# First-layer attention weights: a third exponential, and the remainder taken from the PSUM bank

## The chip, the cores and the metric

The kernel runs on one core of a Trainium2 chip. The metric is device time in microseconds (us) of one execution. The engines that matter are TensorE (PE in the profile, its weight loads PEld), VectorE (DVE), ScalarE (ACT), GpSimd (POOL) and SyncE (SP, which issues the transfers). Each runs its own instructions in the order in which they stand, and waits for others by semaphores. SBUF is the large working memory; PSUM has eight banks, into which TensorE writes its products, here each 128 partitions by 512 fp32 columns.

## The reference, cut to what matters

A two-layer encoder trunk for 2048 new frames and 32 sample frames, 1024 wide, all in fp32. The change lies in layer 0, 16 heads of 64, where a frame sees its own chunk of 64 and the eight chunks before it:

```python
s = jnp.einsum('bqhd,bkhd->bhqk', q, k).astype(jnp.float32) * scale
s = s + bias[None]                                  # clipped relative-position bias
s = jnp.where(mask[None, None], s, NEG_INF)
p = jax.nn.softmax(s, axis=-1).astype(v.dtype)
return jnp.einsum('bhqk,bkhd->bqhd', p, v)
```

Queries and keys are RMS-normalised per head before; the output is gated by silu(z) and projected. Layer 1 (latent attention) follows and is untouched.

## The kernel before

TensorE multiplies operands of a rounded fp32 kind. To keep fp32 accuracy the kernel splits every operand into a high part (rounded) and a low part (the remainder), and issues three products, or two where one side needs no split (`mm3`, lines 187 to 191).

Layer 0 is a run of 32 steps: two halves of the sequence, in each eight groups of two heads, in each two blocks of 512 queries. One step works on scores and values of a (group, block) while the projections, transposes and row maxima of the next are laid between them. `place` gives each piece a position in the step, and a scheduler that builds the program settles the order of the instructions on every engine from its own account of when things are ready; so an edit of one line can move neighbours on all engines.

Scores come in tiles of 128 keys by w queries (w = 128, 256, 384 or 512, each equally often). In block 0 a head has four tiles, in the blocks 1 to 3 eight: 8 groups x 2 heads x (4 + 3 x 8) = 448 tiles, 112 of each width. One tile goes through these steps (`scores`, `values`):

- two matmuls (lines 629 and 630) write the scores into a PSUM bank with the tag `st`. There are two such banks, used in turn (bank_74 and bank_78 in the built program), so tile i+2 needs the bank of tile i;
- VectorE adds the bias in the bank (633 or 636), or writes the mask (637);
- ScalarE takes exp twice from the bank: `P`, fp32 in SBUF (643), and `Ph`, the rounded high part (644);
- VectorE forms the low part `Pl` = `P` - `Ph` (645), all three in SBUF;
- GpSimd adds `P` to the running sum of the row, `acc` (647). For a head's first tile `P` is `acc` itself;
- two matmuls by the values, `Ph` first (656), then `Pl` (657), into a bank with the tag `av`, of which there is one (bank_94). In the program's text they stand two tiles behind the scores (`LAGA`), and the scheduler moves them on.

Beside this, VectorE also takes row maxima (595, 613), reciprocals for the softmax gate (687), splits of weights (429, 441) and of keys and queries (566, 567), and the sums that take the finished values out of the `av` bank (667, after ScalarE's copy 666). ScalarE copies the projections out of their banks (481, 513). In layer 1 a similar tile (`scores` of that layer) adds `P` to a sum that lies in a PSUM bank (1563), or, for a unit's second tile, adds two tiles that lie in SBUF.

Of the kernel before, what the change touches and what calls it, by code (L numbers as in the profile page):

```python
# [10 lines left out]
AF = mybir.ActivationFunctionType  # L11
ALU = mybir.AluOpType
# [19 lines left out]
def f32(ap):  # L32
    return ap if ap.dtype == F32 else ap.bitcast(F32)
# [6 lines left out]
def flip(t, c0, c1):  # L40

    n = t.shape[1]
    a = t[:, n - c1:n - c0]
    return bass.AP(a.tensor, a.offset + c1 - c0 - 1, [list(a.ap[0]), [-1, c1 - c0]])
# [55 lines left out]
def trunk(ctx: ExitStack, tc: tile.TileContext, I, O, stop=99):  # L100
    nc = tc.nc
    V, S, G, T = nc.vector, nc.scalar, nc.gpsimd, nc.tensor
# [90 lines left out]
    def bank(tag):  # L193
        order = psum[tag if tag in psum else "mx"]
        order.append(order.pop(0))
        return banks[order[-1]]
# [144 lines left out]
    def at1(shape, name, dt=F32, bufs=1):  # L341
        return at.tile(shape, dt, tag=name, name=name, bufs=bufs)
# [279 lines left out]
    def scores(s, h, n, c, t):  # L622
        blk, u = s["blk"], s[h]
        src = blk % 2 if c else 1 - blk % 2
        q0, w = (128 * t, 512 - 128 * t) if c else (0, 128 * t + 128)
        ks, qs = slice(128 * t, 128 * t + 128), slice(q0, q0 + w)
        bt = bias[s["g"], h][1]
        st = bank("st")
        T.matmul(st[:, 0:w], KA[h][src][:, ks], u["qa"][:, qs], start=True, stop=False)  # L629
        T.matmul(st[:, 0:w], KG[h][src][:, ks], u["qg"][:, qs], start=False, stop=True)  # L630
        if c:
            b1 = min(256, w)
            V.tensor_tensor(st[:, 0:b1], st[:, 0:b1], flip(bt, 0, b1), ALU.add)  # L633
        else:
            if t == 3:
                V.tensor_tensor(st[:, 0:128], st[:, 0:128], flip(bt, 128, 256), ALU.add)
            V.memset(st[0:64, w - 64:w], NEG)  # L637
        Ph = at1([128, 512], "Ph", F32R, PBUFS)
        Pl = at1([128, 512], "Pl", F32R, PBUFS)
        if n == 0:  # L640
            u["acc"] = at1([128, 512], "acc", bufs=2)
        P = at1([128, 512], "P", bufs=PBUFS) if n else u["acc"]
        S.activation(P[:, 0:w], st[:, 0:w], AF.Exp)  # L643
        S.activation(Ph[:, 0:w], st[:, 0:w], AF.Exp)
        V.tensor_tensor(Pl[:, 0:w], P[:, 0:w], f32(Ph[:, 0:w]), ALU.subtract)
        if n:
            G.tensor_tensor(u["acc"][:, qs], u["acc"][:, qs], P[:, 0:w], ALU.add)  # L647
        return Ph, Pl, w, qs, src
# [289 lines left out]
    for si, s in enumerate(steps):  # L938
# [55 lines left out]
        for i, (h, n, c, t) in enumerate(items):  # L994
            fifo.append((s, h, n, n == len(tiles) - 1, t, scores(s, h, n, c, t)))
            while plan and plan[0][0] <= (i + 1) / len(items):
                next(plan.pop(0)[1], None)
            if len(fifo) > LAGA:
                x = fifo.pop(0)
                values(*x)  # L1000
                if x[3]:
                    evac(x[0], x[1])
# [723 lines left out]
    for i in range(len(items) + LAG + 20):  # L1726
        if i < len(items):
            u, t = items[i]
            fifo.append((u, t, scores(u, t)))
# [233 lines left out]
```

## Time and profile before

| | us |
|---|---|
| median of 3 runs | 3889.08 (3886.15 to 3892.15) |
| profiled execution, device time | 3874.33 |
| its span, first to last instruction | 3872.2 |
| PE busy in the span | 3598.0 (93%) |
| DVE busy | 3023.3 (78%) |
| ACT busy | 2016.7 (52%) |
| POOL busy | 1622.4 (42%) |

The first tile of layer 0 reaches ScalarE at 127 us, and the last tile's work ends at about 1655 us; the stretch 125 to 1655 us is called the stage below. Times in rows are of the one profiled execution. A matmul's duration includes its way through the array: the next one begins before it ends, so busy time of PE is not PE at its peak.

### The profile page before, as it was taken

To read this page: it belongs to the slowest core of one execution; us is meant where nothing else is said; L and a number is where in the kernel's file an instruction comes from. 1 tells how busy PE (TensorE), PEld (TensorE's weight loads), DVE (VectorE), ACT (ScalarE), POOL (GpSimd) and SP (SyncE) were. 2 spreads that over 40 slices of the span, in tenths; PEclk is the share of its full clock that TensorE was granted. 3 is DMA by queue.
4 is the path that set the end of the run, shared out by engine and by line. 5 is a ranking of instruction groups with operands and counts; after the bars stand their busy time and mean duration, and the time that the engine had idled before them with its cause. 6 is when DMAs were issued, how large, how long until landed. Compare 5 with 4: busy or idle time off the path is not lost.

```text
span 3872.2 us, 56118 instructions
## 1 busy us (share of the span) xinstructions
PE 3598.0 (93%) x17410; PEld 2831.9 (73%) x17410; DVE 3023.3 (78%) x6646; ACT 2016.7 (52%) x4854; POOL 1622.4 (42%) x1680
## 2 busy tenths in 40 slices
PE   7899999889999999899999999889999999998999
PEld 4788888767766777677878888666767667766887
DVE  4788988889988888876777766788888888784663
ACT  4444544655544444542234555566766667664542
POOL 0222223333333323441013444377777777774032
PEclk9899999989999999799999999889999999998999
DMA  5222222222233332354453666652323323223253
GB/s 175 64 58 60 72 77 59 78 80 67 63 104 96 94 92 78 117 182 130 131 173 126 194 192 193 177 153 69 84 70 83 87 73 84 61 76 102 88 175 126
DMA packets 445036, 412.96 MB, mean 107 GB/s; under 512 B 72392, under 2 KB 367356, under 8 KB 437696
## 3 DMA queue, kind: packets, MB, share of 16 engines
q1 hardware_dynamic: 444736, 409.37, 36.2%
q8 instruction: 138, 2.26, 0.3%
q14 instruction: 162, 1.33, 0.1%
HBM read 251.72 MB, written 140.10 MB: 101 GB/s over the span
## 4 chain that ended last, share of the span: by engine, by line
PE 61%; DVE 20%; ACT 6%; issue 5%; DMA 4%; POOL 3%; SPq 0%; ACTq 0%; DVEq 0%; POOLq 0%
PE bank L189 10%; PE bank L190 10%; PE bank L191 10%; PE bank L1512 3%; PE bank L1537 3%; PE bank L1539 3%; PE bank L1538 3%; PE bank L1573 2%; PE bank L1572 2%; DVE ez@69_1247 L687 2%; PE bank L1592 1%; PE bank L656 1%; PE bank L657 1%; PE bank L629 1%; PE bank L591 1%
## 5 line engine op out<-in xcount | busy, mean ns | idle before, releaser
L1513 DVE TENSOR_REDUCE mp@319_16907<-bank 128x1 f32<-128x512 f32 (+3 forms) x384 | 235.1, 616 | 63.7 <-PE bank L1512 61.4
L647 POOL TENSOR_TENSOR acc@61_858<-acc@61_858,P@63_885 128x256 f32<-128x256 f32 (+3 forms) x64 | 57.2, 894 | 212.7 <-ACT P@63_885 L643 110.8
L1513 DVE TENSOR_REDUCE mp@320_16908<-bank 128x1 f32<-128x512 f32 (+1 forms) x192 | 115.7, 619 | 20.2 <-PE bank L1512 16.2
L643 ACT ACTIVATE P@63_885<-bank 128x384 f32<-128x384 f32 (+3 forms) x128 | 52.7, 412 | 126.0 <-DVE bank L633 62.1
L647 POOL TENSOR_TENSOR acc@61_858<-acc@61_858,P@64_886 128x256 f32<-128x256 f32 (+3 forms) x64 | 57.4, 898 | 143.4 <-ACT P@64_886 L643 99.7
L687 DVE RECIPROCAL ez@69_1247<-ez@69_1247 128x128 f32<-128x128 f32 x128 | 116.0, 922 | 0.0
L647 POOL TENSOR_TENSOR acc@61_858<-acc@61_858,P@65_887 128x128 f32<-128x128 f32 (+3 forms) x64 | 57.2, 894 | 139.5 <-ACT P@65_887 L643 94.8
L643 ACT ACTIVATE P@65_887<-bank 128x128 f32<-128x128 f32 (+3 forms) x128 | 52.5, 410 | 111.4 <-DVE bank L637 59.1
L1546 ACT ACTIVATE P@432_22141<-bank 128x512 f32<-128x512 f32 (+2 forms) x156 | 83.6, 536 | 49.4 <-PE bank L1539 14.2
L1546 ACT ACTIVATE P@430_22139<-bank 128x512 f32<-128x512 f32 (+2 forms) x156 | 83.7, 537 | 49.0 <-PE bank L1539 15.1
L643 ACT ACTIVATE P@64_886<-bank 128x256 f32<-128x256 f32 (+3 forms) x128 | 52.3, 409 | 108.5 <-DVE bank L633 51.2
L647 POOL TENSOR_TENSOR acc@62_859<-acc@62_859,P@63_885 128x128 f32<-128x128 f32 (+3 forms) x64 | 58.5, 914 | 117.7 <-ACT P@63_885 L643 111.7
L1546 ACT ACTIVATE P@429_22138<-bank 128x512 f32<-128x512 f32 (+2 forms) x156 | 83.8, 537 | 43.5 <-PE bank L1539 17.4
L1546 ACT ACTIVATE P@431_22140<-bank 128x512 f32<-128x512 f32 (+2 forms) x156 | 83.5, 535 | 41.7 <-PE bank L1539 15.5
L647 POOL TENSOR_TENSOR acc@62_859<-acc@62_859,P@65_887 128x256 f32<-128x256 f32 (+3 forms) x64 | 55.1, 862 | 105.1 <-ACT P@65_887 L643 98.9
L647 POOL TENSOR_TENSOR acc@62_859<-acc@62_859,P@64_886 128x256 f32<-128x256 f32 (+3 forms) x64 | 54.7, 855 | 96.9 <-ACT P@64_886 L643 87.0
L149 POOL TENSOR_TENSOR ozl@169_14178<-ozl_@174_14186,ozh@167_14176 128x1024 fp32r<-128x1024 f32 x8 | 19.3, 2410 | 149.9 <-ACT ozh@167_14176 L148 149.7
L1563 DVE TENSOR_TENSOR bank<-bank,P@431_22140 128x512 f32<-128x512 f32 (+2 forms) x108 | 66.8, 619 | 11.6 <-ACT P@431_22140 L1546 9.8
L1563 DVE TENSOR_TENSOR bank<-bank,P@430_22139 128x512 f32<-128x512 f32 (+2 forms) x108 | 66.8, 618 | 11.4 <-ACT P@430_22139 L1546 10.3
L1563 DVE TENSOR_TENSOR bank<-bank,P@429_22138 128x512 f32<-128x512 f32 (+2 forms) x108 | 66.8, 618 | 10.6 <-ACT P@429_22138 L1546 9.0
L1563 DVE TENSOR_TENSOR bank<-bank,P@432_22141 128x512 f32<-128x512 f32 (+2 forms) x108 | 66.7, 618 | 9.1 <-ACT P@432_22141 L1546 8.2
L1547 ACT ACTIVATE Ph@421_22117<-bank 128x512 fp32r<-128x512 f32 (+1 forms) x128 | 72.8, 569 | 0.0
(2154 smaller groups left out, 14826.7 us busy)
## 6 DMA issues: line engine op xcount, KB each, us to landing
h<-hT@197_14210 SPq DMA_DIRECT2D x16, 1024.0 KB
N<-hl@383_17303 SPq DMA_DIRECT2D x32, 512.0 KB
N<-hl@384_17304 SPq DMA_DIRECT2D x32, 512.0 KB
wr@10_289<-in_a_w_in SPq DMA_DIRECT2D x64, 192.0 KB
wr@11_290<-in_a_w_in SPq DMA_DIRECT2D x64, 192.0 KB
xr@9_224<-in_ada_w SPq DMA_DIRECT2D x32, 256.0 KB
xr@8_223<-in_ada_w SPq DMA_DIRECT2D x32, 256.0 KB
h1@214_14229<-h SPq DMA_DIRECT2D x8, 1024.0 KB
```

What stands on the lines that cost most here:

```text
L189: T.matmul(out, lhs[0], rhs[0], start=start, stop=False)
L190: T.matmul(out, lhs[0], rhs[1], start=False, stop=False)
L191: T.matmul(out, lhs[1], rhs[0], start=False, stop=stop)
L643: S.activation(P[:, 0:w], st[:, 0:w], AF.Exp)
L647: G.tensor_tensor(u["acc"][:, qs], u["acc"][:, qs], P[:, 0:w], ALU.add)
L687: V.reciprocal(ez[:, cs], ez[:, cs])
L1512: T.matmul(X[:, 0:w], qz[0:n, js], kz[0:n, 512 * c:512 * c + w], start=True, stop=True)
L1513: V.tensor_reduce(mp[:, j, c:c + 1] if blk else m4[:, j:j + 1], X[:, 0:w], AX.X, ALU.max)
L1537: T.matmul(st[:, 0:w], kz[0:96, ks], ql[:, qs], start=True, stop=False)
L1538: T.matmul(st[:, 0:w], kz[0:n, ks], qz[0:n, qs], start=False, stop=False)
L1546: S.activation(P[:, 0:w], st[:, 0:w], AF.Exp)
L1563: V.tensor_tensor((u["acc"] if last else u["sum"])[:, qs], old, P[:, 0:w], ALU.add)
```

## The change

In `scores` of layer 0, ScalarE takes the exponential a third time, from the `st` bank back into the same place of the bank, and VectorE forms `Pl` from the bank, where it took `P` from SBUF:

```diff
         S.activation(P[:, 0:w], st[:, 0:w], AF.Exp)
         S.activation(Ph[:, 0:w], st[:, 0:w], AF.Exp)
-        V.tensor_tensor(Pl[:, 0:w], P[:, 0:w], f32(Ph[:, 0:w]), ALU.subtract)
+        S.activation(st[:, 0:w], st[:, 0:w], AF.Exp)
+        V.tensor_tensor(Pl[:, 0:w], st[:, 0:w], f32(Ph[:, 0:w]), ALU.subtract)
         if n:
             G.tensor_tensor(u["acc"][:, qs], u["acc"][:, qs], P[:, 0:w], ALU.add)
```

From there on every line number of the changed kernel is one higher: its third exponential is line 645, the subtraction 646, the value matmuls 657 and 658. `P` is now read by GpSimd alone. The `st` bank was free for tile i+2 when ScalarE had taken `Ph`; now it is free when VectorE has subtracted.

The scheduler moves instructions on all engines with it. On VectorE, at the start of a step with eight tiles per head (at about 500 us in the trace): before

```order
L645 TENSOR_TENSOR Pl@60_857<-acc@61_858,Ph@57_854 128x512
L645 TENSOR_TENSOR Pl@58_855<-P@65_887,Ph@55_852 128x512
L637 MEMSET bank_74 64x64
L633 TENSOR_TENSOR bank_78<-bank_78,BT0@37_580 128x256
L592 MEMSET bank_90 64x64
L592 MEMSET bank_82 64x64
L456 TENSOR_SCALAR BQ0@36_579<-BQ0@36_579 128x256
L645 TENSOR_TENSOR Pl@59_856<-P@63_885,Ph@56_853 128x384
```

and now

```order
L646 TENSOR_TENSOR Pl@60_857<-bank_74,Ph@57_854 128x512
L595 TENSOR_REDUCE md@51_695<-bank_90 128x1
L646 TENSOR_TENSOR Pl@58_855<-bank_78,Ph@55_852 128x512
L637 MEMSET bank_74 64x64
L595 TENSOR_REDUCE md@51_695<-bank_82 128x1
L633 TENSOR_TENSOR bank_78<-bank_78,BT0@37_580 128x256
L456 TENSOR_SCALAR BQ0@36_579<-BQ0@36_579 128x256
L613 ISA bank_86,m4@49_693<-bank_86,BQ1@39_589,md@51_695 128x256
L613 ISA m4@49_693 128x1
L646 TENSOR_TENSOR Pl@59_856<-bank_74,Ph@56_853 128x384
```

Row maxima (595, 613) now stand between a tile's bias and its subtraction. Over all 448 tiles there were 1422 VectorE instructions between the two in the order before (3.2 a tile), and 1769 now (3.9 a tile).

On TensorE, shortly behind that place, where the two banks are taken again for tiles of 256 columns: before

```order
L608 MATMUL bank_86<-KG11@31_564,QG@47_608 128x128
L604 MATMUL bank_86<-KG11@31_564,QG@47_608 128x256
L594 MATMUL bank_90<-KG11@31_564,QG@47_608 128x128
L594 MATMUL bank_82<-KG11@31_564,QG@47_608 128x256
L629 MATMUL bank_74<-QA@44_605,KA00@24_557 128x256
L630 MATMUL bank_74<-QG@46_607,KG00@28_561 128x256
L656 MATMUL bank_94<-Ph@56_853,VT00@32_565 128x384
L191 MATMUL bank_66<-wq@19_300,HT0@0_117 128x384
L657 MATMUL bank_94<-Pl@59_856,VT00@32_565 128x384
```

and now

```order
L191 MATMUL bank_70<-wq@13_294,HT0@0_117 128x384
L189 MATMUL bank_70<-wq@14_295,HT0@0_117 128x384
L190 MATMUL bank_70<-wq@14_295,HT0@0_117 128x384
L191 MATMUL bank_70<-wq@14_295,HT0@0_117 128x384
L629 MATMUL bank_74<-QA@44_605,KA00@24_557 128x256
L630 MATMUL bank_74<-QG@46_607,KG00@28_561 128x256
L658 MATMUL bank_94<-Pl@59_856,VT00@32_565 128x384
L657 MATMUL bank_94<-Ph@57_854,VT01@33_566 128x384
L189 MATMUL bank_70<-wq@15_296,HT0@0_117 128x384
```

Projection matmuls (189 to 191) now stand ahead of the scores, and the matmul by `Pl` of the tile that held the bank before stands right behind them: both wait for the same subtraction. In the program before, 44 of the 446 pairs of tiles that share a bank one after the other have fewer than twelve matmuls between them on TensorE, now 5; pairs of score matmuls with a `Pl` matmul directly, or one matmul, behind them are 94 before and 212 now.

## Rows read from the trace of the kernel before

**Rows 1.** Busy time by stretch: us of the stretch, busy us of each engine (instructions).
```profile
core 0: us, PE busy (x) PEld busy (x) DVE busy (x) ACT busy (x) POOL busy (x), PEclk, DMA share, GB/s
125.00:1655.00 1530.00, 1426.72 (x7042) 1137.86 (x7041) 1321.76 (x3178) 750.54 (x1837) 511.27 (x523) 0.96 0.28 80
400.00:600.00 200.00, 192.81 (x1024) 161.23 (x1025) 178.74 (x446) 96.64 (x234) 58.10 (x63) 1.00 0.25 69
800.00:1000.00 200.00, 185.54 (x881) 147.97 (x879) 182.70 (x442) 101.09 (x249) 75.60 (x77) 0.93 0.25 68
```
**Rows 2.** Chain that ended last, shares by line, of 400:600, then of 800:1000.
```profile
by line: PE bank L190 10.9%; PE bank L191 10.5%; PE bank L189 10.3%; DVE ez@69_1247 L687 7.6%; DMA QG@46_607<-QA@44_605 4.1%; PE bank L656 3.5%; issue 3.3%; PE bank L657 3.3%; PE bank L591 3.3%; DVE bank L613 3.1%; DVE Pl@60_857 L645 3.0%; 
...
by line: PE bank L190 8.3%; PE bank L191 8.0%; PE bank L189 7.9%; issue 4.7%; DVE Pl@58_855 L645 4.6%; PE bank L657 4.3%; PE bank L591 4.2%; PE bank L656 3.8%; PE bank L629 2.9%; DVE Pl@59_856 L645 2.8%; DVE Pl@60_857 L645 2.8%; DVE ez@69_1
```
**Rows 3.** Busy time by stretch, of line 645 (the subtraction) alone: DVE busy (instructions).
```profile
125.00:1655.00 1530.00, 323.55 (x448) 0.96 0.28 80
...
800.00:1000.00 200.00, 48.30 (x67) 0.93 0.25 68
400.00:600.00 200.00, 41.38 (x58) 1.00 0.25 69
```
**Rows 4.** Line 645: groups (busy us, mean ns), then one with ns min/median/max.
```profile
L645 DVE TENSOR_TENSOR Pl@59_856<-P@63_885,Ph@56_853 128x384 fp32r<-128x384 f32 x20 | 18.2, 908 | 0.7 <-ACT Ph@56_853 L644 0.3
...
L645 DVE TENSOR_TENSOR Pl@58_855<-P@65_887,Ph@55_852 128x512 fp32r<-128x512 f32 x14 | 14.9, 1067 | 2.2 <-ACT Ph@55_852 L644 2.2
...
L645 DVE TENSOR_TENSOR Pl@59_856<-acc@61_858,Ph@56_853 x5: 692/693/693, 881.0 to 1486.5; 128x512 fp32r<-128x512 f32 x5
```
**Rows 5.** Lines 567 and 1563 (VectorE, tensor by tensor): min/median/max, or busy and mean.
```profile
L567 DVE TENSOR_TENSOR KA00@24_557<-bank,KA00@24_557 x16: 693/693/695, 84.1 to 1516.8; 64x512 fp32r<-64x512 f32 x16
...
L1563 DVE TENSOR_TENSOR bank<-bank,P@431_22140 128x512 f32<-128x512 f32 x84 | 58.4, 695 | 11.3 <-ACT P@431_22140 L1546 9.8
...
L1563 DVE TENSOR_TENSOR bank<-bank,P@432_22141 128x256 f32<-128x256 f32 x12 | 5.1, 421 | 0.0
...
L1563 DVE TENSOR_TENSOR bank<-bank,P@432_22141 128x128 f32<-128x128 f32 x12 | 3.4, 285 | 0.1
...
L1563 DVE TENSOR_TENSOR bank<-P@429_22138,P@430_22139 x12: 546/1202/1443, 2725.9 to 3489.5; 128x384 f32<-128x384 f32 x12
```
**Rows 6.** Exponentials: line 643's ACT busy in the stage, then timeline (start us, us).
```profile
125.00:1655.00 1530.00, 193.31 (x448) 0.96 0.28 80
...
499.58 0.59 ACT L643 ACTIVATE acc@61_858<-bank 128x512 f32<-128x512 f32 x1
500.06 0.60 ACT L644 ACTIVATE Ph@57_854<-bank 128x512 fp32r<-128x512 f32 x1
...
505.03 0.39 ACT L643 ACTIVATE P@65_887<-bank 128x256 f32<-128x256 f32 x1
505.31 0.39 ACT L644 ACTIVATE Ph@55_852<-bank 128x256 fp32r<-128x256 f32 x1
```
**Rows 7.** Line 645: its engine sat idle before it (us, times) until the named ended.
```profile
  ACT Ph@57_854 L644: 17.4, 37
  ACT Ph@55_852 L644: 11.9, 23
  ACT Ph@56_853 L644: 8.4, 16
```
**Rows 8.** Who waited for whom in the stage, TensorE: us in total, times, longest.
```profile
PE bank L656 <- DVE ob@66_1077 L667: 14.5, 7, 2.9
...
PE bank L656 <- DVE ob@67_1078 L667: 11.6, 13, 2.0
...
PEld bank L629 <- ACT Ph@57_854 L644: 15.9, 26, 2.1
PEld bank L629 <- ACT Ph@56_853 L644: 10.0, 28, 1.2
...
PEld bank L629 <- ACT Ph@55_852 L644: 6.1, 16, 0.9
```

## The prediction

> **What bounds the kernel now.** I read the busy times by stretch first. In the stage of layer 0, 1530 us long, TensorE is busy 1426.7 us (93%), VectorE 1321.8 us (86%), ScalarE 750.5 us (49%) and GpSimd 511.3 us (33%) [rows 1]. In the two stretches of 200 us inside it VectorE is at 89% and 91%, TensorE at 96% and 93% [rows 1]. So two engines are nearly full there, and ScalarE has half its time free. The change touches only this stage.
>
> The chain of work that ended last comes next. TensorE's projections lead it, but VectorE is in it again and again, and the subtraction of line 645 with it: in 800:1000 us its three buffers make 4.6 + 2.8 + 2.8 = 10.2% of the stretch, 20.4 us; in 400:600 us one buffer's 3.0%, 6.0 us, is all that the row shows [rows 2]. The line is busy 48.3 us and 41.4 us in these stretches, 323.6 us in the stage [rows 3]. So between 6.0 / 41.4 = 15% and 20.4 / 48.3 = 42% of it lies on the path.
>
> Then the line's own durations. Tiles of equal size differ by far: 692 ns for 512 columns in one group, a mean of 1067 ns in another, 908 ns for 384 columns [rows 4]. The neighbours say why. Line 567, with one input in a bank and one in SBUF, takes 693 to 695 ns each time; line 1563 with the sum in a bank has means of 695, 421 and 285 ns for 512, 256 and 128 columns; the same line with both inputs in SBUF takes 546 to 1443 ns for 384 columns, half of them over 1200 [rows 5]. An input in PSUM keeps the instruction from being slowed, two in SBUF don't, and GpSimd's addition of line 647 starts on the same `P` at about the same time.
>
> **The change part by part.** *VectorE, line 645.* The subtraction now has one input in the bank. At 285, 421 and 695 ns, with 558 ns for 384 columns (halfway between its neighbours), 112 tiles of each width are 112 x 1.959 = 219 us [rows 5] in place of 323.6 us [rows 3]: 104 us of VectorE's time go. No row shows this very instruction (bank and SBUF in, rounded fp32 out); line 567 has the same operands on half the partitions and is the nearest. With the share on the path from above, 15% to 42%, between 15 and 44 us come off the end. I take a third, 35 us, nearer the upper end, since the row of 400:600 us shows one of the three buffers only.
>
> The Trainium skill speaks against this part: Perfetto Trace Analysis, Optimizing Scalar/DVE Operations, gives VectorE an access overhead of about 60 ns on SBUF and 125 ns on PSUM. By it each subtraction would cost some 65 ns more, 448 x 65 ns = 29 us (an estimate from that page), and the time would come out some 10 us higher than my sum, still below the time before. The trace does not bear it out: 693 ns with a bank as one input against 692 ns for a subtraction in SBUF that nobody disturbed [rows 4, 5].
>
> *ScalarE, the third exponential.* One of 512 columns begins 0.48 us before the next, one of 256 columns 0.28 us [rows 6]; so 384 and 128 columns take 0.38 and 0.18 us by the same step, 0.33 us in the mean, 448 x 0.33 = 148 us. The upper bound is a whole duration each, 193 us, as line 643 has in the stage [rows 6]. Writing into PSUM instead of SBUF has no row for an exponential; I take the same. ScalarE goes to 898 us, 59% of the stage (62% at the bound), and stays far from full; of what is queued behind it (copies of projections, of queries, of finished values) I count nothing.
>
> *The subtraction waits one exponential longer.* VectorE sat idle for `Ph` 37 + 23 + 16 = 76 times, 37.7 us [rows 7]; in the other 372 cases it came late itself. With nothing moved, the 76 would each cost 0.33 us more, 25 us. But the order puts 347 more VectorE instructions between bias and subtraction, and one takes 1321.8 us / 3178 = 0.42 us in the mean [rows 1]: 347 x 0.42 / 448 = 0.32 us a tile, the length of the exponential. I count 5 us of the 25. The cover is VectorE's own work (row maxima, for the most part); where it is missing, the 25 us are to pay, and what stands behind on VectorE is the next bias, on which ScalarE waits.
>
> *The bank is held longer.* The next but one score matmul now needs the end of the subtraction, 0.33 us (exponential) + 0.49 us (219 us / 448) later than before. In the trace TensorE's weight load of line 629 waited for `Ph` 26 + 28 + 16 = 70 times, 32.0 us [rows 8]. In the order such matmuls have moved: close reuses of a bank (under twelve matmuls between) fall from 44 to 5, and more of the score matmuls have the `Pl` product right behind them, which waits for the same subtraction anyway. I count nothing; the bounds are 57 us at the upper end (70 x 0.82) and at the lower end the waits for the emptied `av` bank (14.5 + 11.6 = 26 us behind line 667 [rows 8]), which a shorter VectorE queue can shorten.
>
> *GpSimd* loses a neighbour at the SBUF inputs and can begin a head's second tile earlier, as the subtraction no longer reads `acc`. It is busy a third of the stage, so this is worth nothing.
>
> *Sum.* -35 + 5 = -30 us. On the profiled execution's 3874.3 us that is 3844 us. That execution lies 14.8 us below the median of the runs, 3889.1 us, by which the change is measured: 3859 us.
>
> **The rivals.** *Nothing reaches the end.* TensorE is busy 93% of the stage [rows 1]; if its own matmuls carry the time, the 104 us turn into idle time of VectorE. What speaks for it is 96% in 400:600 us; against it that busy matmuls overlap and that the chain holds so much of VectorE. 3889 us, within 8 us.
>
> *The bank decides (slower).* Two `st` banks serve 448 tiles in 1530 us, a tile every 3.4 us, so a bank comes round in 6.8 us in the mean, but tiles come in bursts. If the 70 waits at line 629 stay and each grows by the full 0.82 us, 57 us are added, and with 35 us gained the kernel is 22 us slower: 3911 us. It decides from 35 / 0.82 = 43 such waits at the full price. For it: the waits are there, 70 of them, and the lengthening falls on every tile. Against: the order has spread the tiles.
>
> *The subtraction is slowed all the same.* If its one SBUF input is enough for a collision with GpSimd, the 104 us stay, and the longer wait (25 us) is all that is left: 3894 to 3914 us. Rows 5 speak against it in every width that they show.
>
> **How the numbers follow.** The forecast, -10 to -70 us (3819 to 3879 us): 0.57. Nothing reaches the end: 0.17. The bank decides: 0.20. Slowed all the same: 0.06. About 0.2%, 8 us, is what a measurement of this kernel can tell from no change. Faster by over that: 0.57; within: 0.17; slower: 0.26. The range goes from 3819 us (the upper share of 44 us and the 26 us of the `av` bank) to 3908 us, which takes in the middle case and the cheaper half of the slower ones; some 0.15 are left out above and 0.04 below. The forecast's own range, which holds most of the chance, is 3819 to 3879 us.
>
> **What would show it right or wrong.** Line 646 of the changed kernel at about 220 us in all, with no group above 0.75 us for 512 columns: if not, the first step falls. ScalarE in the stage at about 900 us. VectorE idle for the third exponential (line 645) no more than some 45 us in all: if 60 us or more, the order did not cover it. Waits of lines 629 for VectorE's `Pl` (line 646) no more than 32 us on the weight loads: if they are twice that, the bank decides. The stage, 125 to 1655 us, should end near 1625 us. What would make the prediction wrong above all is a stretch in which tiles come in a burst, so that TensorE, VectorE and ScalarE hand one bank round and none of them has other work in between.

## The result, and the profile after

The changed kernel takes 3845.35 us in the median (3835.06 to 3851.45, 4 runs), the kernel before, run beside it, 3890.61 us (3886.15 to 3901.47, 4 runs). The medians lie 45 us apart. The ratio, taken over all runs, is 0.9877 [0.9845, 0.9909], that is 48 us less (35 to 60; here and below the gain is the ratio, turned into us on 3890 us). The profiled execution of the changed kernel takes 3840.68 us, that of before 3874.33 us.

The code of the change stands one line further down from the subtraction on: line 645 is now the third exponential, 646 the subtraction, 648 GpSimd's addition, 657 and 658 the products with `Ph` and `Pl`, 668 the sum that empties the `av` bank, 669 the row sum of a head.

First the busy times by stretch of the changed kernel, as in [rows 1] (us of the stretch, busy us and instructions of PE, PEld, DVE, ACT and POOL, granted clock, DMA share, GB/s):

```profile
125.00:1655.00 1530.00, 1442.20 (x7216) 1156.78 (x7215) 1256.39 (x3221) 921.59 (x2329) 498.94 (x535) 0.96 0.29 84
...
400.00:600.00 200.00, 189.91 (x1024) 160.39 (x1023) 167.40 (x440) 118.23 (x296) 55.01 (x64) 1.00 0.23 63
800.00:1000.00 200.00, 192.23 (x964) 157.02 (x964) 167.58 (x471) 129.84 (x333) 71.70 (x80) 0.97 0.26 69
```

And the same of line 646 alone (VectorE), then of line 645 alone (ScalarE), as in [rows 3]; all 448 of each lie in this stretch:

```profile
125.00:1620.00 1495.00, 216.21 (x448) 0.96 0.29 83
...
125.00:1620.00 1495.00, 200.34 (x448) 0.96 0.29 83
```

In the same 1530 us more work fits: 7216 matmuls where it was 7042. VectorE falls from 1321.8 to 1256.4 us although it runs 43 instructions more in the stretch. In 400:600 us TensorE runs 1024 matmuls as before, at 800:1000 us 964 instead of 881. The subtraction takes 216.21 us where it took 323.55 us. The third exponential takes 200.34 us of ScalarE.

The tiles of one size are now all alike. These are line 646's instructions by destination buffer (ns minimum, median, maximum, first and last start, shapes), then what VectorE waited for ahead of them and who waited for them:

```profile
L646 DVE TENSOR_TENSOR Pl@58_855<-bank,Ph@55_852 x150: 216/425/692, 130.5 to 1610.9; 128x256 fp32r<-128x256 f32 x45, 128x512 fp32r<-128x512 f32 x38, 128x128 fp32r<-128x128 f32 x38, 128x384 fp32r<-128x384 f32 x29
L646 DVE TENSOR_TENSOR Pl@59_856<-bank,Ph@56_853 x149: 229/548/693, 131.7 to 1606.8; 128x384 fp32r<-128x384 f32 x45, 128x512 fp32r<-128x512 f32 x37, 128x128 fp32r<-128x128 f32 x37, 128x256 fp32r<-128x256 f32 x30
L646 DVE TENSOR_TENSOR Pl@60_857<-bank,Ph@57_854 x149: 228/540/692, 134.3 to 1607.7; 128x384 fp32r<-128x384 f32 x38, 128x256 fp32r<-128x256 f32 x37, 128x512 fp32r<-128x512 f32 x37, 128x128 fp32r<-128x128 f32 x37
its engine sat idle before it (us, times) until:
  ACT bank L645: 52.4, 79
who waited for it (us, times):
  PEld bank L629: 69.7, 82
  PE bank L629: 41.5, 54
```

No instruction is longer than 693 ns, against means of 908 and 1067 ns in groups of before [rows 4]. The last two lines are new: TensorE's next score matmul (629) now waits for the subtraction, because the bank comes free only with it; in the kernel before it waited 32.0 us (weight loads) and 12.1 us (matmuls) for `Ph`. Two more views of waits show what else moved. These are the waits of ScalarE's first exponential for VectorE's mask (637) and bias (633) in the changed kernel, then in the kernel before (us in total, times, longest):

```profile
ACT P@63_886 L643 <- DVE bank L637: 55.1, 44, 3.4
ACT P@65_888 L643 <- DVE bank L637: 47.6, 40, 2.7
ACT P@64_887 L643 <- DVE bank L637: 44.8, 40, 2.7
...
ACT P@63_886 L643 <- DVE bank L633: 42.7, 24, 4.3
ACT P@65_888 L643 <- DVE bank L633: 38.9, 25, 3.4
ACT P@64_887 L643 <- DVE bank L633: 38.8, 24, 3.4
```
```profile
ACT P@63_885 L643 <- DVE bank L633: 62.1, 31, 5.4
...
ACT P@65_887 L643 <- DVE bank L637: 59.1, 37, 4.0
ACT P@63_885 L643 <- DVE bank L637: 57.8, 42, 3.2
ACT P@64_886 L643 <- DVE bank L633: 51.2, 26, 4.4
ACT P@64_886 L643 <- DVE bank L637: 49.4, 37, 2.8
...
ACT P@65_887 L643 <- DVE bank L633: 48.1, 26, 5.1
```

The six waits sum to 327.7 us before and 267.9 us after. That is no proof of a shorter queue on VectorE, because ScalarE, with a third pass, can come to the bank later itself: in e1 below, where the subtraction is as slow as ever and the kernel gains nothing, the same six fall to 294.2 us, and in e5, where it is fast without a third pass, they rise to 344.2 us. TensorE's waits for the emptied `av` bank, 26.1 us on the matmuls before [rows 8], nearly vanish:

```profile
PE bank L657 <- DVE ob@66_1083 L668: 2.3, 2, 1.7
PEld bank L657 <- DVE ob@67_1084 L668: 0.9, 1, 0.9
```

These waits moved rather than went. Every kernel with two banks that subtracts from the bank has almost none of them (on the matmuls 2.5 us in e3, 0.2 in e4, 0.7 in e6 below), while e5, with a subtraction nearly as short but from SBUF, keeps 20.2 us. With weight loads and matmuls together, TensorE waits 44.1 us at the score bank and 62.3 us at the `av` bank before, 111.2 us and 3.4 us after.

Where the time is won and where some of it goes back, two places show. The last row sum of layer 0 (line 668 before, 669 after) and the first matmul of layer 1's row maxima (1512 before, 1513 after), before and then after:

```profile
L668 DVE TENSOR_TENSOR pair@68_1079<-acc@62_859 x32: 689/690/1658, 150.5 to 1655.5; 64x512 f32<-64x512 f32 x32
...
L1512 PE MATMUL bank<-KZ0@311_16899,QZ1@315_16903 x24: 225/399/506, 2484.1 to 2688.0; 96*128 96x512 f32 x16, 100*128 100x128 f32 x2, 100*128 100x256 f32 x2, 100*128 100x384 f32 x2
```
```profile
L669 DVE TENSOR_TENSOR pair@68_1085<-acc@62_859 x32: 689/690/1298, 150.3 to 1612.0; 64x512 f32<-64x512 f32 x32
...
L1513 PE MATMUL bank<-KZ0@311_17347,QZ1@315_17351 x24: 225/399/505, 2450.7 to 2655.9; 96*128 96x512 f32 x16, 100*128 100x128 f32 x2, 100*128 100x256 f32 x2, 100*128 100x384 f32 x2
```

At the end of the stage the changed kernel is 1655.5 - 1612.0 = 43.5 us ahead, at the start of layer 1's attention 2484.1 - 2450.7 = 33.4 us, and that is the difference of the two profiled executions, 33.7 us. So about 10 us go back in the code between the layers, which the change doesn't touch. The profile of the changed kernel has the chain that ended last only from 1336 us on, so [rows 2] has no counterpart, and the experiments have to say how much of the subtraction lay on the path.

### The profile page after: what moved, and what is told of

The parts are those of the page before. It is cut to its first block, busy times and chain, and to the rows that moved or that the text cites. A ratio compares the mean times of both kernels' runs of the same rounds, so it can differ in the third digit from the quotient of the medians.

```text
span 3838.9 us, 56651 instructions
## 1 busy us (share of the span) xinstructions
PE 3579.7 (93%) x17410; PEld 2825.5 (74%) x17410; DVE 2925.8 (76%) x6646; ACT 2171.1 (57%) x5302; POOL 1592.2 (41%) x1680
## 4 chain that ended last, share of the span: by engine, by line
PE 44%; DVE 9%; issue 4%; ACT 3%; DMA 3%; POOL 2%; SPq 0%; DVEq 0%; ACTq 0%; POOLq 0%
PE bank L189 7%; PE bank L190 7%; PE bank L191 7%; PE bank L1513 3%; PE bank L1538 3%; PE bank L1540 3%; PE bank L1539 3%; PE bank L1574 3%; PE bank L1573 2%; PE bank L1593 2%; DVE mp@320_17356 L1514 1%; DVE mp@319_17355 L1514 1%; DVE bank L1564 1%; PE bank L830 1%; PE bank L1424 1%
## 5 line engine op out<-in xcount | busy, mean ns | idle before, releaser
L645 ACT ACTIVATE bank<-bank 128x512 f32<-128x512 f32 x448 | 200.3, 447 | 0.0
L648 POOL TENSOR_TENSOR acc@61_858<-acc@61_858,P@63_886 128x256 f32<-128x256 f32 (+3 forms) x64 | 52.2, 816 | 213.3 <-ACT P@63_886 L643 172.7
L648 POOL TENSOR_TENSOR acc@61_858<-acc@61_858,P@64_887 128x256 f32<-128x256 f32 (+3 forms) x64 | 52.4, 818 | 154.1 <-ACT P@64_887 L643 121.9
L1547 ACT ACTIVATE P@429_22586<-bank 128x512 f32<-128x512 f32 (+2 forms) x156 | 83.7, 537 | 44.1 <-PE bank L1540 20.1
L648 POOL TENSOR_TENSOR acc@61_858<-acc@61_858,P@65_888 128x128 f32<-128x128 f32 (+3 forms) x64 | 51.8, 809 | 130.2 <-ACT P@65_888 L643 104.3
L643 ACT ACTIVATE P@65_888<-bank 128x128 f32<-128x128 f32 (+3 forms) x128 | 52.4, 410 | 87.3 <-DVE bank L637 47.6
L648 POOL TENSOR_TENSOR acc@62_859<-acc@62_859,P@65_888 128x256 f32<-128x256 f32 (+3 forms) x64 | 54.5, 851 | 114.0 <-ACT P@65_888 L643 106.5
L643 ACT ACTIVATE P@64_887<-bank 128x256 f32<-128x256 f32 (+3 forms) x128 | 52.4, 409 | 86.6 <-DVE bank L637 44.8
L648 POOL TENSOR_TENSOR acc@62_859<-acc@62_859,P@63_886 128x128 f32<-128x128 f32 (+3 forms) x64 | 55.0, 859 | 104.2 <-ACT P@63_886 L643 100.6
L648 POOL TENSOR_TENSOR acc@62_859<-acc@62_859,P@64_887 128x256 f32<-128x256 f32 (+3 forms) x64 | 54.2, 848 | 95.1 <-ACT P@64_887 L643 94.8
L646 DVE TENSOR_TENSOR Pl@58_855<-bank,Ph@55_852 128x512 fp32r<-128x512 f32 (+3 forms) x150 | 71.5, 477 | 21.5 <-ACT bank L645 20.2
L646 DVE TENSOR_TENSOR Pl@60_857<-bank,Ph@57_854 128x384 fp32r<-128x384 f32 (+3 forms) x149 | 72.1, 484 | 19.2 <-ACT bank L645 16.8
L646 DVE TENSOR_TENSOR Pl@59_856<-bank,Ph@56_853 128x384 fp32r<-128x384 f32 (+3 forms) x149 | 73.1, 491 | 17.7 <-ACT bank L645 15.4
L1564 DVE TENSOR_TENSOR bank<-bank,P@431_22588 128x512 f32<-128x512 f32 (+2 forms) x108 | 66.7, 618 | 11.4 <-ACT P@431_22588 L1547 9.7
```

Source lines behind the costliest of these rows:

```text
L645: S.activation(st[:, 0:w], st[:, 0:w], AF.Exp)
L646: V.tensor_tensor(Pl[:, 0:w], st[:, 0:w], f32(Ph[:, 0:w]), ALU.subtract)
```

## The experiments

Three theories to begin with. A: the gain is the slowing of the subtraction that is gone, since one input no longer comes from SBUF. B: the gain is the order that the scheduler gave to the changed program, whatever the operands. C: the gain is that `P` and `acc` are read by GpSimd alone and come free sooner. All twelve kernels, with the subtraction's busy time over its 448 tiles; the edits below are shown against the changed kernel, those of e5 and e8 are made to the one before:

| kernel | median us | ratio to before | us against before | subtraction us |
|---|---|---|---|---|
| before | 3890.61 | 1 | 0 | 324.0 |
| after | 3845.35 | 0.9877 [0.9845, 0.9909] | -48 | 216.2 |
| e1, third pass only | 3900.22 | 1.0021 [1.0002, 1.0039] | +8 | 332.9 |
| e2, third pass into SBUF | 3868.20 | 0.9929 [0.9910, 0.9949] | -28 | 272.9 |
| e3, two exponentials | 3851.11 | 0.9887 [0.9860, 0.9915] | -44 | 211.8 |
| e4, `P` last, as a copy | 3850.74 | 0.9885 [0.9861, 0.9909] | -45 | 212.2 |
| e5, before without additions | 3811.10 | 0.9792 [0.9764, 0.9820] | -81 | 225.5 |
| e6, after without additions | 3817.03 | 0.9803 [0.9776, 0.9831] | -77 | 215.7 |
| e7, after with three banks | 3825.96 | 0.9831 [0.9799, 0.9863] | -66 | 215.4 |
| e8, before with three banks | 3894.94 | 1.0010 [0.9980, 1.0040] | +4 | 318.1 |
| e9, three banks, `P` last | 3866.04 | 0.9950 [0.9932, 0.9968] | -19 | 210.1 |
| e10, three banks, lag of three | 3892.72 | 1.0007 [0.9986, 1.0028] | +3 | 214.5 |

**The third pass alone (e1).** The third exponential stays, VectorE subtracts from `P` in SBUF as before; nobody reads what the pass leaves in the bank.

```diff
         S.activation(st[:, 0:w], st[:, 0:w], AF.Exp)
-        V.tensor_tensor(Pl[:, 0:w], st[:, 0:w], f32(Ph[:, 0:w]), ALU.subtract)
+        V.tensor_tensor(Pl[:, 0:w], P[:, 0:w], f32(Ph[:, 0:w]), ALU.subtract)
```

> The changed kernel with one part undone: ScalarE still takes the third exponential into the bank, but VectorE subtracts from P in SBUF, as before. The order of the instructions stays near that of the changed kernel. Theory A (the gain is VectorE's subtraction no longer slowed by GpSimd at the SBUF inputs): line 646 busy again at 300 to 330 us, and the time back at the kernel before or above it, 3890 to 3920 us. Theory B (the gain is the other order that the scheduler made): line 646 does not matter, about 3845 to 3860 us. Theory C (the gain is that P and acc are read by GpSimd alone and come free sooner): VectorE reads them again, so about 3890 us.

It takes 8 us more than before [1.0002, 1.0039], and the subtraction is as slow as ever, 332.9 us. One of its groups (columns as for line 646 above):

```profile
L646 DVE TENSOR_TENSOR Pl@59_856<-P@64_887,Ph@56_853 x48: 269/739/1786, 174.6 to 1642.2; 128x128 fp32r<-128x128 f32 x16, 128x256 fp32r<-128x256 f32 x14, 128x512 fp32r<-128x512 f32 x11, 128x384 fp32r<-128x384 f32 x7
```

So the added instruction, with the order that comes with it, gives nothing. The order of e1 is one of its own, however: between a tile's bias or mask and its subtraction stand 1550 VectorE instructions over all tiles, against 1422 before and 1769 after, so e1 alone does not settle theory B. The runs below do: e3 and e4, with 1385 and 1393 instructions there, gain as much as the change, and e5 and e6, with 1413 and 1724, are level.

Theory C doesn't fit the trace of before. GpSimd's additions waited 138.7 us for the subtraction to let go of `P` and `acc` (who waited for line 645, first two lines), but behind the additions next to nobody waited (who waited for line 647, last line), so freeing them sooner had little to give (and e2 below, where `P` and `acc` are GpSimd's alone, keeps 28 of the 48 us):

```profile
  POOL acc@61_858 L647: 118.3, 27
  POOL acc@62_859 L647: 20.4, 11
...
  DVE pair@68_1079 L668: 0.3, 1
```

**Two SBUF inputs, one of them new (e2).** The third exponential goes into `Pl`'s own place (`twin` is the same memory, read as plain fp32), and VectorE subtracts there. The bank comes free with the exponential, as in e1.

```diff
-        S.activation(st[:, 0:w], st[:, 0:w], AF.Exp)
-        V.tensor_tensor(Pl[:, 0:w], st[:, 0:w], f32(Ph[:, 0:w]), ALU.subtract)
+        S.activation(twin(nc, Pl)[:, 0:w], st[:, 0:w], AF.Exp)
+        V.tensor_tensor(Pl[:, 0:w], twin(nc, Pl)[:, 0:w], f32(Ph[:, 0:w]), ALU.subtract)
```

> The third exponential goes to SBUF, into the place of Pl, and VectorE subtracts Ph from it there: two SBUF inputs, P read by GpSimd alone, the bank free after the third exponential. Theory A (slowed subtraction): line 646 at 300 to 330 us, 3885 to 3915 us. Theory C (P and acc come free sooner): the same as the change, about 3845 us, or better, since the bank comes free sooner.

What A expected missed: the subtraction takes 272.9 us, so only 272.9 - 216.2 = 57 us are lost to slowing, half of what before loses, and the kernel keeps 28 of the 48 us. One of its groups:

```profile
L646 DVE TENSOR_TENSOR Pl@59_856<-Pl_@69_892,Ph@56_853 x149: 270/559/1775, 130.1 to 1639.5; 128x384 fp32r<-128x384 f32 x45, 128x512 fp32r<-128x512 f32 x37, 128x128 fp32r<-128x128 f32 x37, 128x256 fp32r<-128x256 f32 x30
```

A single subtraction still reaches 1775 ns, so two SBUF inputs do collide; but the median is back at 559 ns. That the subtraction, one pass later, runs beside the addition on `P` less is the likely reason: laid over each other in the traces, subtractions and additions (line 648) run at the same time for 160 us in e1 and 106 us in e2. It was not tried by itself. What the pair of e1 and e2 does show is the price: 60 us less of subtraction, with the bank freed by the same instruction in both, are 0.0092 of the ratio, 36 us (32 us by the medians). That is 0.6 us of the end for each us of slowing (0.4 to 0.8 by the intervals). The two differ in the scheduler's order as well (1550 and 1795 instructions between bias and subtraction), so a part of it may be the order's.

**No third pass (e3).** The first exponential is left out; GpSimd adds the rounded `Ph` (or copies it, for a head's first tile). The row sum then leaves out the low parts.

```diff
-        S.activation(P[:, 0:w], st[:, 0:w], AF.Exp)
         S.activation(Ph[:, 0:w], st[:, 0:w], AF.Exp)
         S.activation(st[:, 0:w], st[:, 0:w], AF.Exp)
...
-            G.tensor_tensor(u["acc"][:, qs], u["acc"][:, qs], P[:, 0:w], ALU.add)
+            G.tensor_tensor(u["acc"][:, qs], u["acc"][:, qs], f32(Ph[:, 0:w]), ALU.add)
+        else:
+            G.tensor_copy(P[:, 0:w], f32(Ph[:, 0:w]))
```

> Prices the third ScalarE pass: only two exponentials (the rounded high part to SBUF, then the bank in place); GpSimd adds the rounded high part to the row sum instead of P, so the sum leaves out the low parts. VectorE subtracts from the bank as in the changed kernel. Theory A with a hidden third pass: 3835 to 3848 us, as the changed kernel within 10 us. Rival (the third pass costs by its wait or by ScalarE's load): 15 to 40 us below the changed kernel, 3805 to 3830 us.

ScalarE falls to 768 us in the stage and the kernel is as fast as the changed one (-44 against -48 us, the intervals cover each other):

```profile
125.00:1655.00 1530.00, 1438.88 (x7155) 1161.55 (x7156) 1248.05 (x3205) 768.26 (x1860) 534.36 (x594) 0.95 0.29 82
```

The third pass, some 150 us of ScalarE, costs nothing that can be measured here (the difference is known to some 17 us).

**`P` last (e4).** `Ph` and the exponential in the bank come first, and `P` is copied from the bank; in the program's text the copy stands behind the subtraction.

```diff
-        S.activation(P[:, 0:w], st[:, 0:w], AF.Exp)
         S.activation(Ph[:, 0:w], st[:, 0:w], AF.Exp)
         S.activation(st[:, 0:w], st[:, 0:w], AF.Exp)
         V.tensor_tensor(Pl[:, 0:w], st[:, 0:w], f32(Ph[:, 0:w]), ALU.subtract)
+        S.copy(P[:, 0:w], st[:, 0:w])
```

> Same work as the changed kernel in another order of ScalarE's passes: high part, bank in place, and P last, as a copy out of the bank. VectorE's subtraction can begin one pass sooner; the bank is held until the copy is done. If the wait for the third pass costs something: 5 to 15 us below the changed kernel, 3830 to 3840 us. If VectorE's own queue covers it: the same within 8 us.

VectorE now idles 25.8 us, 64 times, ahead of the subtraction (52.4 us, 79 times after), and the kernel takes the same time, -45 us. This does not price the wait for one exponential more by itself. In none of the 448 tiles does the copy begin before the subtraction has ended; ScalarE sits idle 119.5 us ahead of it, and the score matmul waits for the copy instead (56.0 us on weight loads, 26.3 us on matmuls). So one wait was exchanged for others, and the run shows only that they come out level.

**Without GpSimd's additions (e5 of before, e6 of after).** The additions are left out, and the row sum is the head's first tile plus one.

```diff
-        if n:
-            G.tensor_tensor(u["acc"][:, qs], u["acc"][:, qs], P[:, 0:w], ALU.add)
...
-        V.tensor_tensor(s["pair"][hs, :], u["acc"][0:64, :], u["acc"][64:128, :], ALU.add)
+        V.scalar_tensor_tensor(s["pair"][hs, :], u["acc"][0:64, :], 1.0, u["acc"][64:128, :], ALU.add, ALU.add)
```

> The kernel before without GpSimd's additions of line 647 (the row sum holds a head's first tile alone, plus one): the suspected partner in the collision is taken away, VectorE subtracts in SBUF as before. Theory A: line 645 falls from 324 to about 220 us and the time by as much as the change gave, 3835 to 3860 us. If the change's gain lies elsewhere (ScalarE, the order, the bank): 3880 to 3895 us.

> The changed kernel without GpSimd's additions (the row sum holds a head's first tile alone, plus one). Theory A: nothing is left to gain from that in the subtraction, so 3830 to 3850 us, within 15 us of the changed kernel and at or above the kernel before without the additions. Rival (GpSimd's additions also slow other VectorE work, or their collision was not the point): 20 us or more below the changed kernel.

The stage of e5, then of e6 (columns as in the first fence):

```profile
125.00:1655.00 1530.00, 1448.29 (x7315) 1166.38 (x7315) 1258.83 (x3248) 779.00 (x1903) 205.41 (x154) 0.97 0.31 87
```
```profile
125.00:1655.00 1530.00, 1442.31 (x7333) 1165.68 (x7332) 1250.62 (x3257) 932.99 (x2364) 193.26 (x155) 0.97 0.31 87
```

With the additions gone, the two kernels are level (-81 and -77 us), and the old subtraction, still with two SBUF inputs, takes 225.5 us (GpSimd still does its other work). So the slowing comes from GpSimd's additions, and the change is worth something only beside them. The size agrees with e1 and e2: taking the additions away gives before 81 - 29 = 52 us more than after (the change's 48 us against the 77 us of e6), for 98 us less of subtraction, 0.53 us per us (0.3 to 0.7 by the intervals).

The miss is e6: the changed kernel, whose subtraction isn't slowed, still gains 29 us from the missing additions (12 to 45 by the intervals), twice the bound that was expected. The changed kernel has a wait that e6 has not, VectorE's row sum for a head's last addition; in the kernel before it was 0.3 us, once:

```profile
DVE pair@68_1085 L669 <- POOL acc@62_859 L648: 13.6, 21, 1.1
```

The rival that was named beside e6's expectation, that the additions slow other VectorE work too, is in the traces. The gate's product, with two SBUF inputs (line 689 in the changed kernel, 687 in e6), takes 946 ns in the median with the additions and 683 ns without:

```profile
L689 DVE TENSOR_TENSOR z@53_827<-z@53_827,ez@69_1258 x16: 677/946/1786, 181.3 to 1581.6; 128x512 f32<-128x512 f32 x16
...
L687 DVE TENSOR_TENSOR z@53_827<-z@53_827,ez@69_1250 x16: 676/683/1208, 180.6 to 1557.6; 128x512 f32<-128x512 f32 x16
```

Over the lines of layer 0 that both kernels run equally often, VectorE is busy some 21 us less in e6. How the 29 us divide between this and the 13.6 us of waiting stays open.

**Three banks (e7 of after, e8 of before).** One of the three banks of the tag `mx` (row maxima and transposes) goes to `st`.

```diff
-    psum_pool(mm=2, st=2, mx=3, av=1)
+    psum_pool(mm=2, st=3, mx=2, av=1)
```

> The changed kernel with three score banks instead of two, and two instead of three for row maxima and transposes. In the changed kernel TensorE's line 629 waits 41.5 us idle for the subtraction. If the bank's longer hold costs: the wait falls to under 10 us and the time to 3815 to 3835 us. If the two remaining banks for maxima bind instead: 3845 to 3900 us.

> The kernel before with the same division of banks, as the control for the run with three score banks: its score banks were free early, so little is to be had from a third one: 3885 to 3920 us.

With the change a third bank takes the kernel to 3825.96 us, the best of all; the kernel before gains nothing from it. In e7 the waits of the score matmul for the subtraction are nearly gone (69.7 and 41.5 us after). These are the two lines for who waited for line 646 (us, times):

```profile
  PEld bank L629: 9.8, 11
  PE bank L629: 5.8, 10
```

The three kernels that hold two banks until the subtraction or later (after, e3, e4) lie at 0.9877 to 0.9887, 0.9883 in the mean; e7 is 0.0052 below, 20 us (6 to 34). That is the price of the longer hold in this mix, with the order that the scheduler gave to three banks (2118 instructions between bias and subtraction) included. e7's own profiled execution (3834.86 us) shows the stage ending earlier still, and more of it going back between the layers:

```profile
L669 DVE TENSOR_TENSOR pair@68_1085<-acc@62_859 x32: 687/689/1250, 152.2 to 1592.9; 64x512 f32<-64x512 f32 x32
...
L1513 PE MATMUL bank<-KZ0@311_17347,QZ1@315_17351 x24: 225/398/501, 2444.9 to 2649.7; 96*128 96x512 f32 x16, 100*128 100x128 f32 x2, 100*128 100x256 f32 x2, 100*128 100x384 f32 x2
```

It is 62.6 us ahead of before at the end of layer 0 and 39.2 us at the start of layer 1's attention. What takes the 23 us was not tried.

**Two attempts to go on from there (e9, e10).** e9 puts e4's order on three banks, e10 lets the values lie three tiles behind the scores where it was two.

```diff
-    LAGA = 2
+    LAGA = 3
```

> The changed kernel with three score banks and ScalarE's pass for P last, as a copy out of the bank. If, with the bank no longer short, the wait for the third pass is what is left: 3810 to 3820 us, below the run with three banks alone. If it is covered by VectorE's queue, as with two banks: 3820 to 3832 us, the same.

> The changed kernel with three score banks and the value matmuls three tiles behind the scores in the program's text instead of two. If TensorE's waits for the subtraction at the value matmuls still cost: 3810 to 3822 us. If three buffers of Ph and Pl bind first, or the scheduler gives the same order: 3822 to 3845 us.

Both missed. In e10 four tiles are under way with three buffers of `Ph` and `Pl`, so that products read the weights of a newer tile (445 of the 448 products by `Pl` have another width than the tile last written there). They stand closer to the subtraction that they read, not farther: 0.63 us in the median from its end, against 2.10 us in e7. So a longer lag was not tried. e9 loses 47 us against e7. The largest wait that it has and e7 has not is that of ScalarE's copy (line 646) for the subtraction (645), 102.6 us of idle time, as in e4. Others that it has, or has more of, the last line being one part of that wait:

```profile
ACT ez_@70_1259 L676 <- DVE pair@68_1085 L669: 36.2, 23, 3.7
...
DVE pair@68_1085 L669 <- POOL acc@62_859 L648: 19.1, 16, 1.7
...
ACT Ph@56_853 L643 <- PE bank L657: 18.3, 6, 3.1
...
ACT P@63_886 L646 <- DVE Pl@60_857 L645: 14.9, 17, 2.0
```

The copy of `P` comes later than the exponential did, and the additions, row sums and buffers behind it with it. Whether these waits or the scheduler's other order are the cause stays open.

## Why the prediction was right, point by point

It said 3859 us, a gain of 30 us by the slowed subtraction, and the time is 3845.35 us, inside the forecast's own range of 3819 to 3879. The mechanism is the one that was named, and the runs show it (e1, e2, e5). The sum came out 14 us short, and two of its terms were off by about 20 us each, in opposite directions; that the total came so near is in part luck.

**The subtraction's own time** was right: 219 us predicted, 216.2 measured, and no instruction over 0.75 us. The sentence from the Trainium skill (Perfetto Trace Analysis, Optimizing Scalar/DVE Operations), by which each would cost 65 ns more, would have made it 219 + 29 = 248 us (an estimate from that page); the trace of after does not agree.

**What of it lies on the path** was the first mis-sized term. A third of 104 us was taken, 15% to 42% being the bounds from the chain [rows 2, 3]. The chain of the whole stage gives that third as well: added up, it holds 108.6 us of the line's 323.6. But the pairs that isolate the slowing give 0.6 (e1 and e2) and 0.53 (e5 and e6, against before and after), so 55 to 65 us and not 35; their intervals reach down to the prediction's upper bound of 42%. So here the chain's share of the line probably understates what its shortening was worth. One part of the reason is that the slowed subtractions lie on the chain more often than the others: of what the 448 last longer than tiles of their width after, about 43% is in subtractions that the chain holds (an estimate, tile by tile from the two traces). The rest stays open. The waits do not explain it: ScalarE's for bias and mask fall in e1 too, without a gain, and TensorE's for the `av` bank moved to the score bank.

**The bank held longer** was the second. It was counted at nothing, on the ground that the order spreads the tiles. The own test of the prediction, weight-load waits for the subtraction of no more than 32 us and "if they are twice that, the bank decides", came out at 69.7 us. So the wait is there in full, and the price that e7 takes back is about 20 us (6 to 34), a third of the upper bound of 57 us. It did not decide, since the gain was larger as well. The step that failed is the one that read a changed distance of reuse in the order as a free bank.

**The subtraction's longer wait** (25 us at most, 5 counted) came out between the two marks set for it: 52.4 us and 79 times against 37.7 us and 76 times [rows 7], 15 us more. Its price at the end is not to be seen: e4 halves that idle time at the same time of the kernel. But e4 exchanges one hold of the bank for another and lets ScalarE wait for the subtraction, so this shows only that these together come out level.

**ScalarE** was right: 921.6 us in the stage against 898 predicted (the same stretch now holds some of what used to follow it: e3, with two passes, has 768.3 us there where before has 750.5), and e3, which takes a pass away again, is no faster.

**GpSimd** sooner by itself was worth nothing, as predicted: 0.3 us of waiting hung on its additions before. What the prediction didn't have is what they still cost the changed kernel, 29 us (e6): they slow other VectorE instructions with two SBUF inputs, and VectorE's row sum now waits 13.6 us for the last addition.

**The end of the stage** was expected near 1625 us and came at about 1612 us; then some 10 us went back before layer 1's attention.

Together: -55 to -65 us for the slowing and +20 for the bank make -35 to -45 us, against the 48 us (35 to 60) that were measured; the intervals of the two terms cover the difference. The rivals that nothing reaches the end and that the subtraction is slowed all the same are excluded by the ratio's interval and by line 646; the bank's rival had its mechanism right and its price too high.

## What to carry to other kernels

Compare instructions of one shape before anything else: where equal tiles of VectorE with two SBUF inputs differ by a factor of two while GpSimd runs beside them, and ones with a bank as an input do not, moving an input into PSUM can pay, even at the price of one more pass on an engine that has room; here it was worth about half of the lost time. An input that stays in PSUM holds its bank longer: look for the matmul that now waits for the last reader, and give that tag another bank in the same edit (here 20 us more, and nothing without the change). Don't take the chain's share of a line as an upper bound for what shortening it can bring: here it was a third, and the runs gave more than half. And when a wait vanishes, look where it went before counting it as a gain.

## What the runs showed of the hardware

- A VectorE subtraction with a bank and an SBUF tile as inputs is not slowed by GpSimd: 216 to 693 ns over 448 tiles of 128 to 512 columns, while the same with two SBUF inputs reaches 1786 ns (e1). In the changed kernel 287 of the 448 run beside one of GpSimd's additions, and none is longer than 693 ns. The Trainium skill states it so (SBUF — State Buffer, Who interferes with whom: an instruction with at most one SBUF input doesn't contend with GpSimd, one with two contends with GpSimd's reads), and the runs agree, e5 from the other side: without GpSimd's additions two SBUF inputs cost 225.5 us in all. With the subtraction one ScalarE pass later, about half of the slowing is left (e2); that its timing is the cause was not shown.
- An exponential that writes into the bank is slightly longer than one that writes into SBUF. These are line 645 and two groups of line 643 in the changed kernel (busy us, mean ns):

```profile
L645 ACT ACTIVATE bank<-bank 128x512 f32<-128x512 f32 x112 | 68.7, 614 | 0.0
L645 ACT ACTIVATE bank<-bank 128x256 f32<-128x256 f32 x112 | 43.8, 391 | 0.0
...
L643 ACT ACTIVATE acc@61_858<-bank 128x512 f32<-128x512 f32 x32 | 19.0, 595 | 1.6 <-DVE bank L633 1.2
L643 ACT ACTIVATE P@64_887<-bank 128x256 f32<-128x256 f32 x38 | 14.6, 384 | 34.1 <-DVE bank L633 18.9 <-DVE bank L637 15.2
```

- GpSimd's 384 additions cost the changed kernel 29 us although its subtraction isn't slowed (e6); other VectorE instructions with two SBUF inputs are (line 689 above).
